# S5 layer's gated GEMM: last four tiles from plain fp32 to three fp32r products, two of their weight casts on GpSimd

## The chip, the cores and the metric

The kernel runs on one core of one Trainium2 chip. The metric is the device time of one execution in microseconds (us); smaller is better. A core has TensorE (matmuls, PE), VectorE (DVE), ScalarE (ACT), GpSimd (POOL) and SyncE (SP, which here issues most DMAs). Each engine takes its instructions in the order in which the program has them, and waits on semaphores for the others.

## The reference

Two layers on 256 tokens of width 2048: the first with differential attention, the second with an S5 state-space mixer, each followed by an MLP with squared relu. The change is in the S5 mixer's last step, the gated GEMM:

```
def s5_mixer(h, ..., d_skip, w_glu):
    ...                                   # complex diagonal scan over the sequence, giving y
    y = y + d_skip.astype(F32) * h.astype(F32)
    g = jax.nn.gelu(y).astype(h.dtype)
    val, gate = jnp.split(g @ w_glu, 2, axis=-1)
    return val * jax.nn.sigmoid(gate)
```

All is fp32. `g` is 256 x 2048 and `w_glu` 2048 x 4096.

## The kernel before

**Weights.** All weights come as one stream of chunks of 256 rows by 512 columns (512 KB, a tile `raw` of 128 x 2 x 512, five buffers). Elsewhere in the kernel a GEMM is made of fp32r products: `prep(i)` has ScalarE cast a chunk to fp32r (`wh`, L191), has VectorE subtract to get the remainder (`wl`, L113), and starts the next load with `load_next()`. `ktile` then makes three matmuls of each 128-row tile: high by high, high by low, low by high (L201 to L203). `wh` and `wl` have four buffers each.

**S5 stage.** `s5_phase` loops over 16 tiles of 128 channels. For tile j+1, `s5_e` makes matmuls on TensorE (L1040) and a chain of ten VectorE instructions, two of them scans (L1050), which gives the state `xp`. For tile j, `s5_y` makes the output matmuls on TensorE (L1073), then 16 gelu instructions on ScalarE (L1080), then the cast of `g` to fp32r into `blk.h` (L1084). Groups of `s5_y` are pairs of tiles but for the first two and the last two: (12,13), (14,), (15,). `s5_rest(j)` has VectorE subtract to get the low part `blk.l` of all groups up to j (in the trace a subtraction `x<-s2k,x` of L113); before the change it has lagged three tiles, and the last groups came after the last tile.

**The gated GEMM's first column block.** Inside this loop `glu_tile(j)` multiplies tile j of `g` with rows of `w_glu` for the first 512 columns of `val` (chunk `GLU0 + j//2*2`) and of `gate` (the chunk after it), for two halves of the tokens, into four PSUM accumulators. It takes `g` and `raw` as they are, in plain fp32 (L1106): four matmuls a tile, each of which the trace records as two. The order of work is written out by hand: tiles 0 to 12 are done inside the loop, three iterations behind (tile 12 in iteration 15), and 13, 14 and 15 after it. The other three column blocks follow as ordinary GEMMs of fp32r products, `gemm(glu_lhs)`, beginning with chunk GLU0+16. Between them `evict_val` copies the `val` accumulators (L1298) and `evict_gate` takes the sigmoid (L1305) and adds to the residual, which TensorE then transposes for the next MLP (L445).

Of the kernel before, what the change touches and what calls it, by code (L numbers as in the profile page):

```python
# [16 lines left out]
P = 128  # L17
# [5 lines left out]
KB = 4  # L23
# [14 lines left out]
NJ = 16  # L38
# [2 lines left out]
SLOTS_HOP = 3  # L41
WARM = (18, 4, 8)
LAG = 3


class Lhs:
# [11 lines left out]
def tile_trunk(  # L58
# [8 lines left out]
    act = nc.scalar  # L67
    pe = nc.tensor
    pool_e = nc.gpsimd
# [10 lines left out]
    def nm(s):  # L80
        uid[0] += 1
        return f"{s}_{uid[0]}"
# [15 lines left out]
    def bank():  # L98
        return ring("sd")

    def tmp(shape, tag, bufs=None, dt=F32):
        if bufs is None:
            return sb.tile(shape, dt, tag=tag, name=nm(tag))
        return sb.tile(shape, dt, tag=tag, name=nm(tag), bufs=bufs)
# [7 lines left out]
    def sub(o, a, b):  # L112
        v.tensor_tensor(out=o, in0=a, in1=b, op=ALU.subtract)  # L113

    def tsc(o, a, s1, op0, s2=None, op1=None):
        if op1 is None:
            v.tensor_scalar(out=o, in0=a, scalar1=s1, scalar2=None, op0=op0)
        else:
            v.tensor_scalar(out=o, in0=a, scalar1=s1, scalar2=s2, op0=op0, op1=op1)
# [11 lines left out]
    def pump():  # L131
        clock[0] += 1
        for g in list(side):
            if g[0] <= clock[0]:
                try:
                    d = next(g[1])
                    g[0] = clock[0] + (d if d else 1)
                except StopIteration:
                    side.remove(g)

    def until(cond):
        while not cond():
            assert side
            pump()


    stream = []
# [12 lines left out]
    raws, preps = {}, {}  # L160
    pos = [0]
    FINE = 2
    GLU0 = (12 + 4 + 32) * 8
    POOL = 6

    def load(i):
        if i >= len(stream) or i in raws:
            return
        r = wp.tile([P, WK, BW], F32, tag="raw", name=nm("raw"), bufs=RAW)
        if i < FINE:  # L170
            for k in range(WK):
                nc.sync.dma_start(r[:, k], stream[i][:, k])
        else:
            nc.sync.dma_start(r, stream[i])
        raws[i] = r

    def load_next():

        load(len(raws))

    def prep(i):
        if i >= len(stream) or i in preps or GLU0 <= i < GLU0 + 16:
            return
        r = raws[i]
        h = wp.tile([P, WK, BW], F32R, tag="wh", name=nm("wh"), bufs=LIVE)
        l = wp.tile([P, WK, BW], F32R, tag="wl", name=nm("wl"), bufs=LIVE)
        preps[i] = (h, l)
        step = 1 if i < FINE else WK
        for k in range(0, WK, step):
            sl = slice(k, k + step)  # L190
            act.copy(h[:, sl], r[:, sl])  # L191
            if FINE <= i < POOL:
                sub(l[:, 0], r[:, 0], h[:, 0].bitcast(F32))
                pool_e.tensor_tensor(out=l[:, 1], in0=r[:, 1], in1=h[:, 1].bitcast(F32), op=ALU.subtract)
            else:
                sub(l[:, sl], r[:, sl], h[:, sl].bitcast(F32))
        load_next()

    def ktile(accs, lhs, k, wh, wl, t, first, last):
        ts = slice(t * P, (t + 1) * P)  # L200
        pe.matmul(accs[t], lhs.h[:, k, ts], wh, start=first, stop=False)  # L201
        pe.matmul(accs[t], lhs.h[:, k, ts], wl, start=False, stop=False)  # L202
        pe.matmul(accs[t], lhs.l[:, k, ts], wh, start=False, stop=last)  # L203

    def ahead():
        for d in range(AHEAD + 1):
            prep(pos[0] + d)
# [16 lines left out]
    def new_accs():  # L224
        return [ring("acc") for _ in range(NT)]
# [94 lines left out]
    def keep_warm(n):  # L320

        if n == 0:
            return
        a = ring("acc")
        for _ in range(n):
            pe.matmul(a, x1[3].h[:, 0, 0:P], x1[3].h[:, 0:2], start=True, stop=True)
# [647 lines left out]
    glu_lhs = [Lhs() for _ in range(NB)]  # L974
    tab, U, X, G = {}, {}, {}, {}
    first_vals = []

    def s5_fetch(j):

        if j >= NJ or j in tab:  # L980
            return
        tag = "x" if j < 3 else "a"
        teo = lp.tile([P, 2, 2, Q, P], F32, tag=tag, name=nm("teo"))
        te, to = teo[:, 0], teo[:, 1]
        t2 = tmp([P, SCR - O_T], "t4", bufs=4)
        nc.sync.dma_start(te.rearrange("p i q c -> p (i q c)"), scr[j][:, O_E:O_O])
        nc.sync.dma_start(to.rearrange("p i q c -> p (i q c)"), scr[j][:, O_O:O_T])
        nc.sync.dma_start(t2, scr[j][:, O_T:])
        tab[j] = (te, to, t2[:, 0:Q * P].rearrange("p (q c) -> p q c", q=Q),
                  t2[:, Q * P:].rearrange("p (i q k) -> p i q k", i=2, q=Q))  # L990
# [11 lines left out]
    def s5_dk(j):  # L1002
        if j < NJ:
            act.copy(dks[j % 4][:, :, 1:], rr[:, j * Q:(j + 1) * Q, None].broadcast_to([P, Q, NCH - 1]))
# [22 lines left out]
    def s5_scale(j, factor):  # L1027
        u = U[j]
        uv = u.rearrange("p i q k -> p (i q) k")
        mult(uv, uv, factor[:, None, :].broadcast_to([P, 2 * Q, NCH]))  # L1030
        U[j], U[j + 1] = u[:, 0], u[:, 1]
# [59 lines left out]
    def s5_rest(j):  # L1091

        while rest and rest[0][0] <= j:
            _, blk, kk, n, g = rest.pop(0)
            sub(blk.l[:, kk:kk + n], g[:, 0:n], blk.h[:, kk:kk + n].bitcast(F32))
            blk.ready = kk + n == KB
# [2 lines left out]

    def glu_tile(j):  # L1100

        g = G.pop(j)
        c, kk = GLU0 + j // WK * 2, j % WK
        for i, accs in ((c, A["v"]), (c + 1, A["g"])):
            for t in range(NT):
                pe.matmul(accs[t], g[:, t * P:(t + 1) * P], raws[i][:, kk], start=j == 0, stop=j == NJ - 1)  # L1106
            if j == NJ - 1 and i == c:
                first_vals.extend(evict_val(accs))
            if kk == WK - 1:
                load_next()  # L1110
                pos[0] += 1

    def s5_phase(norm):
        until(lambda: norm.done)
        act.activation(warm_act, warm_act, AF.Gelu_apprx_tanh)
        keep_warm(WARM[0])
        sel = wp.tile([P, 2, NT, P], F32, tag="wl", name="sel", bufs=LIVE)
        ar, diag = sel[:, 0], sel[:, 1]
        for t in range(NT):
            tsc(ar[:, t], sela.rearrange("p s r -> p (s r)"), norm.rstd[:, t:t + 1], ALU.mult)  # L1120
            act.activation(diag[:, t], ident, AF.Copy, scale=norm.rstd[:, t:t + 1])
        prs = bank()[:, 0:NCH]
        for t in range(NT):
            pe.matmul(prs, ar[:, t], selb[:, t], start=(t == 0), stop=(t == NT - 1))
        keep_warm(WARM[1])
        s5_scale(0, prs)
        s5_scale(2, prs)
        s5_e(0)
        for j in (4, 6):
            for _ in s5_u(j, diag, "acc"):  # L1130
                pass
        groups = [(0,), (1,), (2, 3), (4, 5), (6, 7), (8, 9), (10, 11), (12, 13), (14,), (15,)]
        ys = {}
        for grp in groups:
            gen = s5_y(grp)
            for j in grp:
                ys[j] = (gen, j == grp[-1])
        glu = 0
        for j in range(NJ):
            if j + 1 < NJ:  # L1140
                s5_e(j + 1)
            s5_rest(j - 3)
            if j < 2:
                keep_warm(WARM[2])
            if j in (2, 3) or j >= 2 + LAG:
                if glu == 0:
                    A["v"], A["g"] = new_accs(), new_accs()
                glu_tile(glu)
                glu += 1
            gen, end = ys[j]  # L1150
            next(gen)
            s5_dk(j + 4)
            if end:
                for _ in gen:
                    pass
            if j in (2, 4, 6, 8):
                for _ in s5_u(j + 6, diag):
                    pass
            s5_fetch(j + 4)
            pump()  # L1160
        while glu < NJ:
            prep(GLU0 + 16 + glu - NJ + LAG)
            glu_tile(glu)
            glu += 1
        s5_rest(NJ)


    x0 = [Lhs() for _ in range(NB)]
# [1 line left out]
    for b in range(NB):  # L1170
        spawn(xT_block(x0[b], b, 0, norm0, wait=10), 3 * b)
    pump()
    prep(0)
    until(lambda: x0[0].ready)

# [118 lines left out]
    def evict_val(accs):  # L1294
        vs = []
        for t in range(NT):
            n = tmp([P, BW], "vsb", bufs=4)
            act.copy(n, accs[t])  # L1298
            vs.append(n)
        return vs  # L1300
# [75 lines left out]
```

## Time and profile before

| | us |
|---|---|
| median of 3 runs | 2105.34 (2104.72 to 2105.79) |
| the profiled execution | 2103.02 |
| its span, first to last instruction | 2101.2 |
| PE busy (share of the span) | 2076.6 (99%) |
| DVE busy | 1372.2 (65%) |
| ACT busy | 1059.8 (50%) |
| POOL busy | 123.1 (6%) |

Shares of busy time are means over the whole program. What the change is worth is read in the S5 stage, about 1130 to 1250 us, from what each engine waits for there.

### The profile page before, as it was taken

How to read it: one execution, taken by the hardware profiler on the slowest of the kernel's cores; microseconds unless marked ns; L12 is line 12 of the kernel's file. 1: busy time of each engine (PE TensorE's matmuls, PEld its weight loads, DVE VectorE, ACT ScalarE, POOL GpSimd, SP SyncE). 2: the span in 40 equal slices, each digit the busy share in tenths (PEclk: the TensorE clock that was granted, in tenths of full speed). 3: DMA queues.
4: the chain of work that ended last, by engine and by line, in shares of the span. 5: the costliest groups of instructions: out<-in, count | busy, mean ns of one | idle time of the engine just before them, and what ended most of it. 6: DMA issues, size and time to landing. Idle time of an engine off the chain costs nothing.

```text
span 2101.2 us, 31797 instructions
## 1 busy us (share of the span) xinstructions
PE 2076.6 (99%) x12126; PEld 1763.2 (84%) x12126; DVE 1372.2 (65%) x2310; ACT 1059.8 (50%) x1634; POOL 123.1 (6%) x210
## 2 busy tenths in 40 slices
PE   8999999999999999999999999999999999999998
PEld 8899998888888888888887658888888888888886
DVE  5775656688678767767866865565546645645655
ACT  6445545555445544454565874444434434434443
POOL 2000200021020002100110000000000000000000
PEclk9999999999999999999999999999999999999999
DMA  7467765687776777677677855566565556555653
GB/s 249 157 194 237 251 179 178 215 234 266 237 244 224 280 236 224 229 269 233 215 268 296 288 204 190 191 202 197 191 194 189 189 191 191 182 200 180 201 191 130
DMA packets 230813, 452.57 MB, mean 215 GB/s; under 512 B 20818, under 2 KB 29348, under 8 KB 230660
## 3 DMA queue, kind: packets, MB, share of 16 engines
q1 hardware_dynamic: 218400, 416.34, 59.7%
q0 software_dynamic: 11440, 32.86, 4.8%
q8 instruction: 95, 1.56, 0.3%
q10 hardware_dynamic: 820, 1.34, 0.2%
q14 instruction: 58, 0.48, 0.1%
HBM read 420.85 MB, written 41.68 MB: 220 GB/s over the span
## 4 chain that ended last, share of the span: by engine, by line
PE 94%; DVE 2%; DMA 2%; ACT 1%; issue 0%; SPq 0%; ACTq 0%
PE acc L265 21%; PE acc L201 16%; PE acc L203 16%; PE acc L202 16%; PE acc L269 11%; PE acc L248 3%; PE acc L250 3%; PE acc L249 3%; PE acc L1106 2%; PE y L1073 1%; DVE wl L113 1%; ACT s2k L1080 1%; PE sd L1040 1%; DMA raw<-in_mlp_w_dram 1%; PE sd L445 0%
## 5 line engine op out<-in xcount | busy, mean ns | idle before, releaser
L113 DVE TENSOR_TENSOR wl<-raw,wh 128x1024 fp32r<-128x1024 f32 (+1 forms) x690 | 833.2, 1217 | 580.2 <-ACT wh L191 575.6
L191 ACT CAST wh<-raw 128x1024 fp32r<-128x1024 f32 (+1 forms) x690 | 713.4, 1047 | 639.4 <-PE acc L203 351.3
L201 PE MATMUL acc<-wh,x 128*128 128x512 f32 x832 | 326.8, 393 | 0.0
L203 PE MATMUL acc<-wh,x 128*128 128x512 f32 x832 | 324.0, 389 | 0.0
L202 PE MATMUL acc<-wl,x 128*128 128x512 f32 x832 | 323.9, 389 | 0.0
L265 PE MATMUL acc<-x,wh 128*128 128x512 f32 x1024 | 273.9, 394 | 2.3 <-DVE s2k L110 2.3
L265 PE MATMUL acc<-a,wh 128*128 128x512 f32 x1024 | 272.8, 393 | 0.0
L201 PE MATMUL acc<-wh,a 128*128 128x512 f32 x640 | 251.4, 393 | 0.0
L203 PE MATMUL acc<-wh,a 128*128 128x512 f32 x640 | 249.3, 389 | 0.0
L202 PE MATMUL acc<-wl,a 128*128 128x512 f32 x640 | 249.2, 389 | 0.0
L265 PEld LDWEIGHTS acc<-x,wh 128*128 128x128 f32 x1024 | 177.2, 189 | 28.5 <-DVE s2k L110 2.7
L265 PEld LDWEIGHTS acc<-a,wh 128*128 128x128 f32 x1024 | 177.3, 189 | 25.3 <-ACT s2k L1305 0.4
L203 PEld LDWEIGHTS acc<-wh,x 128*128 128x128 f32 x832 | 156.1, 188 | 32.7
L202 PEld LDWEIGHTS acc<-wl,x 128*128 128x128 f32 x832 | 156.2, 188 | 32.2 <-issue 0.2
L201 PEld LDWEIGHTS acc<-wh,x 128*128 128x128 f32 x832 | 156.2, 188 | 32.0 <-ACT vsb L1298 0.2
L269 PEld LDWEIGHTS acc<-a,wl 128*128 128x128 f32 x1024 | 152.8, 190 | 18.7
L269 PEld LDWEIGHTS acc<-x,wl 128*128 128x128 f32 x1024 | 152.4, 190 | 18.8
L269 PE MATMUL acc<-x,wl 128*128 128x256 f32 x1024 | 158.0, 282 | 0.0
L269 PE MATMUL acc<-a,wl 128*128 128x256 f32 x1024 | 157.5, 281 | 0.0
L248 PE MATMUL acc<-x,wh 128*128 128x256 f32 x512 | 148.4, 290 | 1.2 <-ACT wh L191 1.2
L250 PE MATMUL acc<-x,wl 128*128 128x256 f32 x512 | 145.5, 284 | 0.0
L249 PE MATMUL acc<-x,wh 128*128 128x256 f32 x512 | 145.4, 284 | 0.0
(242 smaller groups left out, 2107.9 us busy)
## 6 DMA issues: line engine op xcount, KB each, us to landing
raw<-in_mlp_w_dram SPq DMA_DIRECT2D x512, 512.0 KB
raw<-in_a_w_in_dram SPq DMA_DIRECT2D x94, 512.0 KB
raw<-in_b_w_glu_dram SPq DMA_DIRECT2D x64, 512.0 KB
raw<-in_a_w_out_dram SPq DMA_DIRECT2D x32, 512.0 KB
scr<-t POOLq DMA_DIRECT2D x32, 512.0 KB, 5.7
teo<-scr SPq DMA_DIRECT2D x32, 512.0 KB
t<-scr SPq DMA_DIRECT2D x16, 512.0 KB
pwr<-pwn SPq DMA_DIRECT2D x16, 256.0 KB
```

Of the source, the lines that this page charges most:

```text
L113: v.tensor_tensor(out=o, in0=a, in1=b, op=ALU.subtract)
L191: act.copy(h[:, sl], r[:, sl])
L201: pe.matmul(accs[t], lhs.h[:, k, ts], wh, start=first, stop=False)
L202: pe.matmul(accs[t], lhs.h[:, k, ts], wl, start=False, stop=False)
L203: pe.matmul(accs[t], lhs.l[:, k, ts], wh, start=False, stop=last)
L248: pe.matmul(o, wh[:, kk, cs], lhs.h[:, k], start=f and c % 2 == 0, stop=False)
L249: pe.matmul(o, wh[:, kk, cs], lhs.l[:, k], start=False, stop=False)
L250: pe.matmul(o, wl[:, kk, cs], lhs.h[:, k], start=False, stop=e and c % 2 == 1)
L265: pe.matmul(a[c], wh, lhs.hl[:, k].rearrange("p i s -> p (i s)"), start=first, stop=False)
L269: pe.matmul(a[c][:, S:], wl, lhs.h[:, k], start=False, stop=last)
L1040: pe.matmul(pe_[h, i, q], te[:, i, q, h], u[:, q], start=True, stop=True)
L1106: pe.matmul(accs[t], g[:, t * P:(t + 1) * P], raws[i][:, kk], start=j == 0, stop=j == NJ - 1)
```

## The change

Tiles 12 to 15 of the first column block are done as fp32r products (48 matmuls by `ktile` in place of 16 plain ones). For that, chunks GLU0+12 to GLU0+15 go through `prep`: 12 and 13 at the end of iteration 13, 14 and 15 at the end of iteration 15, the casts of the latter two on GpSimd. `s5_rest` runs one tile less late in the last iteration, and ahead of each tile after the loop. The `prep` of chunks 16 to 18 moves from ahead of tiles 13 to 15 to behind them. The next load is now started by `prep` for the four chunks, not by the tile.

```diff
@@ prep
-        if i >= len(stream) or i in preps or GLU0 <= i < GLU0 + 16:
+        if i >= len(stream) or i in preps or GLU0 <= i < GLU0 + WHOLE:
...
-            act.copy(h[:, sl], r[:, sl])
+            if GLU0 + 14 <= i < GLU0 + 16:
+                pool_e.tensor_copy(h[:, sl], r[:, sl])
+            else:
+                act.copy(h[:, sl], r[:, sl])
@@ glu_tile
-        g = G.pop(j)
+        g, blk = G.pop(j), glu_lhs[j // KB]
...
-                pe.matmul(accs[t], g[:, t * P:(t + 1) * P], raws[i][:, kk], start=j == 0, stop=j == NJ - 1)
+                if i in preps:
+                    wh, wl = preps[i]
+                    ktile(accs, blk, j % KB, wh[:, kk], wl[:, kk], t, j == 0, j == NJ - 1)
+                else:
+                    pe.matmul(accs[t], g[:, t * P:(t + 1) * P], raws[i][:, kk], start=j == 0, stop=j == NJ - 1)
...
-                load_next()
+                if i in preps:
+                    del preps[i]
+                else:
+                    load_next()
@@ s5_phase, loop over j
-            s5_rest(j - 3)
+            s5_rest(j - 3 if j < NJ - 1 else j - 2)
...
             s5_fetch(j + 4)
+            if j == 13:
+                for i in (12, 13):
+                    prep(GLU0 + i)
+            if j == NJ - 1:
+                for i in (14, 15):
+                    prep(GLU0 + i)
             pump()
         while glu < NJ:
+            s5_rest(glu)
+            glu_tile(glu)
             prep(GLU0 + 16 + glu - NJ + LAG)
-            glu_tile(glu)
             glu += 1
-        s5_rest(NJ)
```

`WHOLE` is 12. In the changed file the lines of these functions stand 4 to 18 lower.

First place: VectorE, behind the state chain of tile 14 (whose last instruction writes `bc_11353`). The rows before are the chain of tile 15, which ends with the two writes of `bc_11357`, then the low part of `g` for tiles (10,11), then the remainders of chunks 16 and 17.

```order
L110 TENSOR_TENSOR bc_11353<-s2k_12906,s2k_12907 128x4x63
L107 TENSOR_TENSOR c_2268_12976<-sd_12959,t_2251_12812 128x512 x2
L110 TENSOR_TENSOR c_2268_12976<-c_2268_12976 128x256
L113 TENSOR_TENSOR c_2268_12976<-c_2268_12976 128x256
L1050 SCALAR_TENSOR_TENSOR s2k_12981<-s1k_11356,c_2268_12976 128x256 x2
L107 TENSOR_TENSOR s2k_12984<-s2k_12981,t_2251_12812 128x8x63
L107 TENSOR_TENSOR s2k_12985<-s2k_12981,t_2251_12812 128x8x63
L113 TENSOR_TENSOR bc_11357<-s2k_12984,s2k_12985 128x4x63
L110 TENSOR_TENSOR bc_11357<-s2k_12984,s2k_12985 128x4x63
L113 TENSOR_TENSOR x_12655<-s2k_12793,x_12655 128x2x256
L113 TENSOR_TENSOR wl_13090<-raw_12997,wh_13089 128x1024
L113 TENSOR_TENSOR wl_13104<-raw_13093,wh_13103 128x1024
```

Of the change, the same place: the remainders of chunks 12 and 13 (`wl_12960`, `wl_12966`) stand ahead of the chain of tile 15, which is otherwise the same.

```order
L111 TENSOR_TENSOR bc_11353<-s2k_12906,s2k_12907 128x4x63
L114 TENSOR_TENSOR wl_12960<-raw_12700,wh_12959 128x1024
L114 TENSOR_TENSOR wl_12966<-raw_12850,wh_12965 128x1024
L108 TENSOR_TENSOR c_2274_12988<-sd_12971,t_2251_12812 128x512 x2
L111 TENSOR_TENSOR c_2274_12988<-c_2274_12988 128x256
L114 TENSOR_TENSOR c_2274_12988<-c_2274_12988 128x256
L1054 SCALAR_TENSOR_TENSOR s2k_12993<-s1k_11356,c_2274_12988 128x256 x2
L108 TENSOR_TENSOR s2k_12996<-s2k_12993,t_2251_12812 128x8x63
L108 TENSOR_TENSOR s2k_12997<-s2k_12993,t_2251_12812 128x8x63
L114 TENSOR_TENSOR bc_11357<-s2k_12996,s2k_12997 128x4x63
L111 TENSOR_TENSOR bc_11357<-s2k_12996,s2k_12997 128x4x63
```

Second place: VectorE right behind that chain, of the change. `x_12655` is the low part for tiles (10,11); `x_12957` are those of (12,13), of 14 and of 15; the `wl` rows are the remainders of chunks 14, 15, 16, 17 and 18 in turn. Before, the three rows of `x_12957` stood behind the remainder of chunk 18.

```order
L114 TENSOR_TENSOR x_12655<-s2k_12793,x_12655 128x2x256
L114 TENSOR_TENSOR x_12957<-s2k_12940,x_12957 128x2x256
L114 TENSOR_TENSOR wl_13111<-raw_12854,wh_13110 128x1024
L114 TENSOR_TENSOR wl_13117<-raw_12963,wh_13116 128x1024
L114 TENSOR_TENSOR wl_13135<-raw_12969,wh_13134 128x1024
L114 TENSOR_TENSOR x_12957<-s2k_13036,x_12957 128x256
L114 TENSOR_TENSOR wl_13154<-raw_13005,wh_13153 128x1024
L114 TENSOR_TENSOR x_12957<-s2k_13092,x_12957 128x256
L114 TENSOR_TENSOR wl_13177<-raw_13009,wh_13176 128x1024
```

The low part for tile 14 now has the remainder of chunk 16 ahead of it, and that for tile 15 the remainder of chunk 17.

Third place: ScalarE, of the change, from the gelu of pair (12,13) on. The first two `L195` rows are the casts of chunks 12 and 13, which were not there before; the others are chunks 16, 17 and 18.

```order
L1084 ACTIVATE s2k_12940<-y_12856 32x128 x16
L1088 CAST x_12957<-s2k_12940 128x2x256
L195 CAST wh_12959<-raw_12700 128x1024
L195 CAST wh_12965<-raw_12850 128x1024
L1084 ACTIVATE s2k_13036<-y_13011 32x64 x16
L1088 CAST x_12957<-s2k_13036 128x256
L1084 ACTIVATE s2k_13092<-y_13067 32x64 x16
L1088 CAST x_12957<-s2k_13092 128x256
L195 CAST wh_13134<-raw_12969 128x1024
L195 CAST wh_13153<-raw_13005 128x1024
L1316 COPY vsb_13166<-acc_11991 128x512
L1316 COPY vsb_13168<-acc_11992 128x512
```

Behind these come the cast of chunk 18 and then the table load for the sigmoid; before, all three casts stood ahead of the two copies.

## Rows read from the trace of the kernel before

**Rows 1.** The page's chain that ended last: share of the span by engine.

```profile
PE 94%; DVE 2%; DMA 2%; ACT 1%; issue 0%; SPq 0%; ACTq 0%
```

**Rows 2.** Waits of PE, whole span: waited for, us in total, times, longest.

```profile
PE acc L1106 <- ACT s2k L1080: 4.5, 3, 2.2
```

**Rows 3.** Timeline of PE, 1195 to 1270 us: start, duration, what, idle before.

```profile
1224.66 0.34 PE L1073 MATMUL y<-vsb,t 128*64 128x64 f32 x4
...
1232.93 3.70 PE L1106 MATMUL acc<-raw,s2k 128*128 128x512 f32 x8 [0.54 <-ACT s2k L1080]
...
1238.11 10.57 PE L1106 MATMUL acc<-raw,s2k 128*128 128x512 f32 x24
...
1248.75 0.39 PE L202 MATMUL acc<-wl,x 128*128 128x512 f32 x1
...
1253.28 0.55 PE L445 MATMUL sd<-ident,xres 128*128 128x128 f32 x3 [1.00 <-DVE xres L110]
...
1262.34 0.39 PE L201 MATMUL acc<-wh,x 128*128 128x512 f32 x1
...
1269.82 0.39 PE L201 MATMUL acc<-wh,x 128*128 128x512 f32 x1
```

**Rows 4.** Timeline of ACT, 1214 to 1262 us.

```profile
1226.33 6.55 ACT L1080 ACTIVATE s2k<-y 32x128 f32<-32x128 f32 x16 [4.99 <-PE y L1073]
1232.91 0.62 ACT L1084 CAST x<-s2k 128x512 fp32r<-128x512 f32 x1
...
1238.60 4.59 ACT L1080 ACTIVATE s2k<-y 32x64 f32<-32x64 f32 x16
...
1243.53 1.99 ACT L191 CAST wh<-raw 128x1024 fp32r<-128x1024 f32 x2
...
1249.85 1.09 ACT L1305 ACTIVATE s2k<-acc 128x512 f32<-128x512 f32 x2
```

**Rows 5.** Timeline of DVE, 1214 to 1262 us.

```profile
1215.04 1.29 DVE L107 TENSOR_TENSOR c<-sd,t 128x512 f32<-128x512 f32 x2 [0.75 <-PE sd L1040]
...
1220.32 0.68 DVE L113 TENSOR_TENSOR x<-s2k,x 128x512 fp32r<-128x512 f32 x1
...
1227.26 1.29 DVE L107 TENSOR_TENSOR c<-sd,t 128x512 f32<-128x512 f32 x2 [0.75 <-PE sd L1040]
...
1232.75 0.69 DVE L113 TENSOR_TENSOR x<-s2k,x 128x512 fp32r<-128x512 f32 x1
1244.60 2.36 DVE L113 TENSOR_TENSOR wl<-raw,wh 128x1024 fp32r<-128x1024 f32 x2 [11.16 <-ACT wh L191]
...
1248.62 1.36 DVE L113 TENSOR_TENSOR x<-s2k,x 128x512 fp32r<-128x512 f32 x3
```

**Rows 6.** Groups of POOL by line: busy us, mean ns, idle before.

```profile
L194 POOL TENSOR_TENSOR wl<-raw,wh 128x512 fp32r<-128x512 f32 x4 | 7.1, 1781 | 15.2 <-ACT wh L191 15.2
...
L1332 POOL TENSOR_TENSOR xres<-xres,vsb 128x512 f32<-128x512 f32 x2 | 2.5, 1268 | 992.7 <-ACT junk L421 992.7
```

**Rows 7.** Windows of 1 us: engines' busy us, PEclk, DMA share, GB/s.

```profile
1230.00:1231.00 1.00, 1.00 (x8) 0.24 (x9) 0.97 (x3) 0.98 (x3) 0.00 (x0) 1.00 0.77 246
...
1234.00:1235.00 1.00, 1.00 (x4) 0.47 (x3) 0.00 (x0) 0.95 (x5) 0.00 (x0) 1.00 0.28 96
```

**Rows 8.** Timeline of PE, 0 to 32 us, and 1134 to 1160 us.

```profile
7.65 0.58 PE L248 MATMUL acc<-x,wh 128*128 128x256 f32 x1 [1.25 <-ACT wh L191]
...
10.04 0.41 PE L248 MATMUL acc<-x,wh 128*128 128x256 f32 x1
10.25 0.41 PE L249 MATMUL acc<-x,wh 128*128 128x256 f32 x1
...
11.88 0.28 PE L250 MATMUL acc<-x,wl 128*128 128x256 f32 x1
12.00 0.28 PE L248 MATMUL acc<-x,wh 128*128 128x256 f32 x1
...
1150.18 3.70 PE L1106 MATMUL acc<-raw,s2k 128*128 128x512 f32 x8 [1.81 <-ACT s2k L1080]
```

More of the change, by code (lines that the diff above doesn't have):

```diff
@@ L43 @@
 LAG = 3
+WHOLE = 12
 class Lhs:
```

## The prediction

> **What bounds the kernel now.** I read the chain that ended last first: 94% of it is TensorE [rows 1]. So the kernel is a stream of matmuls, and only two things can move it: how long TensorE computes, and how long it waits. The list of its waits comes next. In the S5 stage before the change it waits for little: 4.5 us in all for gelu results, the longest 2.2 us [rows 2]. Then I read the timelines of TensorE, ScalarE and VectorE from 1214 to 1262 us, where the changed tiles lie. I count tiles from 0 to 15. In the loop over j, tile 12 runs in iteration 15, and tiles 13, 14 and 15 follow the loop. The reader is to see three things. TensorE starts tile 12 at 1232.93, after 0.54 us of waiting, and tiles 13 to 15 at 1238.11 without a wait. The next block's second product starts at 1248.75 [rows 3]. ScalarE is full from 1226.33 on: the gelu of pair (12,13) takes 6.55 us, then its cast, the gelus of 14 and of 15, and at 1243.53 the first weight cast [rows 4]. VectorE runs the state chain of tile 15 from 1227.26, so that it is over soon after 1232.75, and then has nothing until 1244.60 (11.16 us idle) [rows 5].
>
> **What TensorE saves.** A plain fp32 tile takes four matmuls of 512 columns, each recorded as two. Tiles 13 to 15 end, for the product that follows, at 1248.75 − 0.23 = 1248.52: (1248.52 − 1238.11)/3 = 3.47 us each [rows 3]. Tile 12 took about the 3.63 us that its 3.70 us row leaves as pitch. In three parts a tile is 12 fp32r matmuls. Their pitch is (1269.82 − 1262.34)/33 = 0.2267 us, from the first and last of 34 products in a row [rows 3], so 2.72 us. Four tiles: 14.04 − 10.88 = 3.2 us less computing. That is the whole gain on offer, 0.15% of the time; a measurement of this kernel can tell about 0.2% (4.2 us) from no change.
>
> **What the change adds in front of tile 12.** Work for chunks 12 and 13 is written at the end of iteration 13, behind the gelu of (12,13). Both engines take their work in order. So:
>
> 1. ScalarE casts 12 and 13 after the pair's own cast, which starts at 1232.91 and takes 0.62: from 1233.53 on [rows 4]. Two casts take 1.99 us, and VectorE's first subtraction starts 1.07 us after the first cast does (1243.53 to 1244.60) [rows 4, 5]. So the subtraction of chunk 12 starts at 1234.61, however early its weights landed.
> 2. On VectorE both subtractions stand ahead of the state chain of tile 15. The two take 2.36 us, with 0.05 of overlap into the next, 2.3 us [rows 5]. The chain therefore starts at about 1236.9 instead of 1227.26; behind the waiting subtraction its ten instructions stand still for nearly ten microseconds.
> 3. The chain takes 5.28 us up to the subtraction behind it (1215.04 to 1220.32, the same chain of an earlier tile) [rows 5]: 1242.2. Next are the low parts of g for tiles (10,11) and then, moved up one iteration, for (12,13): 128x512 each, 1.36 us for the two by the three of 1248.62, where one is 128x512 and two are half that [rows 5]. They end at 1243.5, call it 1243.6 with the hand-over.
> 4. Tile 12 needs that low part in its third matmul. TensorE can do the first two at 1234.6 and 1235.8, and then stands until 1243.6. Before, tile 12 had begun at 1232.93.
>
> **From there to tile 15.** Ten matmuls remain in tile 12: 2.27 us, to 1245.9. The output matmuls of tile 15 come behind them on TensorE. The gelu starts 1.67 us after such a group (1224.66 to 1226.33) [rows 3, 4], so at 1247.55. From its start to the next weight cast on ScalarE is 4.93 us (1238.60 to 1243.53) [rows 4]: chunk 16 is cast at 1252.5. Here the second wait lies. On VectorE the subtraction of chunk 16 now stands ahead of the low part of g for tile 14, because that chunk is prepared right after tile 13. It starts at 1253.55 and takes 1.15 us, the low part (half of 0.69) about 0.4 us: 1255.15. TensorE is through the outputs by the time that the gelu starts, finishes tile 13 at 1247.5 + 2.72 = 1250.2, does two matmuls of tile 14, and waits some 4.5 us. Tile 15's own low part, behind chunk 17's subtraction, is there by 1256.7 and its third matmul only comes at 1257.9, so it waits no more. From tile 14's third matmul to the next block's second product are 23 pitches, 5.2 us: 1260.36 against 1248.75, **11.6 us later**, gain of the faster tiles included.
>
> **Smaller terms.** The cast of chunk 18 now stands between the copies of the first accumulators and the sigmoid's table load. Before, the sigmoid ran at 1249.85, 1.33 us after tile 15's end [rows 4]. Now: copies end 0.3 us before the end of tile 15, cast 1.05, table load 1.28, so the sigmoid starts 2.0 us after. TensorE waits on that path already (1.00 us at its second transpose [rows 3]), so the 0.7 us count in full. The loads of chunks 15 and 16 leave as before, when tile 11 gives their buffers free. Those of 17 to 20 wait on subtractions instead of tiles; 17 and 18 leave earlier than before (1236 against about 1241). No byte is added and no DMA wait is on the path, so I cost this at nothing; if weights were late again, the cover would be the subtractions that are queued anyway.
>
> **GpSimd's casts.** No row shows a GpSimd cast. The nearest are its 128x512 subtraction, 1.78 us, and a 128x512 product, 1.27 us [rows 6]; for 128x1024 between nothing and 3.56 us. Chunk 15 comes with 16 in the traffic that begins by 1230 and is over before 1235 [rows 7]. The cast is then done by 1238.6 at the latest, and VectorE wants it at 1243.6: hidden. What it may do to VectorE is another matter. GpSimd's subtractions, which the code issues in one breath with a VectorE subtraction of the same size, take 0.51 us longer than its products at the end of the program [rows 6]. The Trainium skill (SBUF — State Buffer, Who interferes with whom) says that a VectorE instruction with two SBUF inputs and a GpSimd instruction that reads SBUF exclude each other, the later one waiting. The 0.51 us agree. By that rule a long cast of chunk 15 would hold the subtraction of chunk 12, which is on the path. I take 0, since chunk 15 is the first of the two loads and VectorE has nothing to do just then, and keep 3.6 us as the upper end. Chunk 14's cast comes beside the chain of tile 14, whose result TensorE wants only about 4 us after the chain's end.
>
> **TensorE's clock after a stand of 7.8 us.** The nearest answer in the middle of the program: after 1.81 us of waiting a tile runs its 3.70 us as ever [rows 8], so nothing. The other end is the start of the program: the 256-column products stand 0.21 us apart at 10.04 and 0.12 apart at 11.88 [rows 8], which are the levels 1.2 and 2.4 GHz. The slow stretch begins with the first product at 7.65 and ends between 10.25 and 11.88 [rows 8]; taken to 11.4, it is 3.7 us of work in which half is lost, 1.9 us. The long stand, with two single matmuls in it, is nearer to the start than to 1.8 us: I take 1.9. The second, 4.5 us, is nearer to 1.8: I take 0 and keep 1.9. The Trainium skill (TensorE: Matmul & The Clock Gate, Why this matters for your kernels) warns against idle gaps between bursts of matmuls, since the clock falls to half. By that rule both stands would cost; no row before shows it in the middle of the program.
>
> **Sum.** 11.6 + 0.7 + 1.9 = 14.2 us. The profiled execution took 2103.02 us (span 2101.2); it would be 2117.2. It is 2.3 us below the median of the runs, 2105.34, and I put the difference on the median: **2119.5 us**, 0.67% slower.
>
> **Rivals.**
> - *Clock never falls:* 12.3 us, 2117.6. For it: no wait in the S5 stage has shown a fall. Chance 0.22.
> - *Clock falls at both stands:* 16.1 us, 2121.4. For it: both are longer than any wait that a row shows at full pace. Chance 0.22. The rule of the Trainium skill on the clock, named above, would give this case.
> - *GpSimd's cast holds VectorE* for its upper end on the path: 14.2 + 3.6 = 17.8 us, 2123.1. Against it: VectorE idles when the chunk lands. Chance 0.06. The rule of the Trainium skill on the shared port, named above, is this case.
> - *No second wait:* if the low part of tile 14 came before chunk 16's subtraction, only the gelu of tile 15 would be late. Its cast ends at 1252.6, its low part at 1253.0, eleven pitches later the next block's second product: 1255.5, so 6.7 + 0.7 + 1.9 = 9.3 us, 2114.6. Against it stands the order on VectorE. Chance 0.04.
> - *Not slower:* the split of chunks 12 and 13 keeps nothing waiting, and 3.2 − 0.7 = 2.5 us are gained: 2102.8. It is decided by ScalarE: its casts would have to be over when the chain of tile 14 leaves VectorE, near 1226.6, about 9 us before they can be. Every microsecond that the two casts come earlier gives one back. Nothing in the profile speaks for it but VectorE's 11.16 us of idleness, which lies too late. Chance 0.04.
>
> **How the numbers follow.** One fall of the clock keeps 0.42 and gives the predicted time. The range 2114.5 to 2123.5 holds every case but the last, with room for a microsecond of spread and for a slow stretch that is longer than at the start. Not slower is 0.04 by the last rival, mostly within 0.2%, since 2.5 us are below it; I leave 0.02 for a gain I don't see.
>
> **What would show it.** In the changed profile: a wait of TensorE at its third fp32r matmul of tile 12 of about 8 us, ended by VectorE; VectorE's subtraction at 1234.6 with an idle stretch of some 8 us before it and the chain of tile 15 behind it; a second wait of 4 to 5 us in tile 14; pitches near 0.45 us behind the first stand if the clock fell; no such pitches behind the second. Wrong would be the prediction if VectorE began that chain near 1227, or if weight casts came before the gelu of (12,13).

## The result and the profile after

| | before | changed |
|---|---|---|
| median, us (4 runs each) | 2105.57 (2104.72 to 2106.74) | 2121.55 (2120.68 to 2122.01) |
| ratio to before | | 1.007, 95% interval 1.0058 to 1.0083 |
| profiled execution, us (span) | 2103.02 (2101.2) | 2121.49 (2119.7) |
| granted TensorE clock, mean | 0.998 | 0.995 |

The changed kernel is slower by 16.0 us between the medians, or 0.8%; by the ratio's interval it is 0.6 to 0.8%. The forecast was 14.2 us. In the changed file all lines named here stand one or more lower, so L113 is L114, L203 is L207 and so on.

TensorE's waits from 1200 to 1275 us in the changed kernel: who waited, for whom, us in total, times, longest.

```profile
PE acc L207 <- DVE x L114: 11.3, 2, 7.1
PE acc L205 <- ACT wh L195: 2.1, 1, 2.1
PE sd L449 <- DVE xres L111: 1.9, 2, 1.0
PE acc L206 <- DVE wl L114: 0.8, 1, 0.8
```

Its timeline on TensorE in the same place. The first row is the state matmuls of tile 15, which stood at 1226.11 before: the trace is 3.09 us late already when it comes here. That difference arose where the two programs still do the same: 1.63 us of it were there at tile 0 (1151.81 against 1150.18 [rows 8]), and the other 1.46 come at tile 2, shown below.

```profile
1229.20 1.10 PE L1044 MATMUL sd<-vsb,teo 128*64 128x64 f32 x32
...
1237.56 0.49 PE L205 MATMUL acc<-wh,x 128*128 128x512 f32 x1 [2.07 <-ACT wh L195]
1238.82 0.49 PE L206 MATMUL acc<-wl,x 128*128 128x512 f32 x1 [0.77 <-DVE wl L114]
1246.43 0.79 PE L207 MATMUL acc<-wh,x 128*128 128x512 f32 x1 [7.12 <-DVE x L114]
1247.02 0.63 PE L205 MATMUL acc<-wh,x 128*128 128x512 f32 x1
1247.44 0.63 PE L206 MATMUL acc<-wl,x 128*128 128x512 f32 x1
...
1250.66 0.34 PE L1077 MATMUL y<-vsb,t 128*64 128x64 f32 x4
...
1255.31 0.39 PE L206 MATMUL acc<-wl,x 128*128 128x512 f32 x1
1259.93 0.50 PE L207 MATMUL acc<-wh,x 128*128 128x512 f32 x1 [4.23 <-DVE x L114]
...
1266.86 0.39 PE L206 MATMUL acc<-wl,x 128*128 128x512 f32 x1
...
1271.75 0.55 PE L449 MATMUL sd<-ident,xres 128*128 128x128 f32 x3 [1.00 <-DVE xres L111]
```

The reader sees both stands (a stand is a longer wait of TensorE): 7.12 us at the third product of tile 12 and 4.23 us at the third product of tile 14, each ended by a low part of g from VectorE. Behind the first the products stand 0.43 us apart instead of 0.23. From the state matmuls to 1266.86, the next block's second product, are 37.66 us; before it was 22.64 (1226.11 to 1248.75 [rows 3]). To the second transpose it is 42.55 against 27.17 us: 15.4 us of the 16.0 are here. The spans of the two profiled executions differ by 18.5 us; the 3.09 and these 15.38 make 18.47 of it, so next to nothing is lost behind.

VectorE in the same stretch:

```profile
1227.54 1.93 DVE L108 TENSOR_TENSOR s2k<-s2k,t 128x504 f32<-128x504 f32 x2
...
1229.84 0.41 DVE L111 TENSOR_TENSOR bc<-s2k,s2k 128x252 f32<-128x252 f32 x1
1237.54 2.36 DVE L114 TENSOR_TENSOR wl<-raw,wh 128x1024 fp32r<-128x1024 f32 x2 [7.28 <-ACT wh L195]
1239.81 1.28 DVE L108 TENSOR_TENSOR c<-sd,t 128x512 f32<-128x512 f32 x2
...
1245.09 1.29 DVE L114 TENSOR_TENSOR x<-s2k,x 128x512 fp32r<-128x512 f32 x2
...
1258.31 1.23 DVE L114 TENSOR_TENSOR wl<-raw,wh 128x1024 fp32r<-128x1024 f32 x1 [9.67 <-ACT wh L195]
1259.45 0.42 DVE L114 TENSOR_TENSOR x<-s2k,x 128x256 fp32r<-128x256 f32 x1
```

It is idle for 7.28 us with the state chain of tile 15 queued behind a subtraction that waits for ScalarE, and for 9.67 us with the low part of tile 14 queued behind chunk 16. Before, that chain began right behind its matmuls [rows 5]. What it waits for is on ScalarE:

```profile
1229.42 6.49 ACT L1084 ACTIVATE s2k<-y 32x128 f32<-32x128 f32 x16 [4.97 <-PE y L1077]
1235.94 0.62 ACT L1088 CAST x<-s2k 128x512 fp32r<-128x512 f32 x1
1236.46 1.99 ACT L195 CAST wh<-raw 128x1024 fp32r<-128x1024 f32 x2
...
1252.32 4.57 ACT L1084 ACTIVATE s2k<-y 32x64 f32<-32x64 f32 x16 [8.84 <-PE y L1077]
1256.93 0.40 ACT L1088 CAST x<-s2k 128x256 fp32r<-128x256 f32 x1
1257.24 1.99 ACT L195 CAST wh<-raw 128x1024 fp32r<-128x1024 f32 x2
```

The casts of 12 and 13 come behind the gelu of their pair, as ordered, and chunk 16's behind the gelu of 15, which itself waited for tile 12. Windows of the changed kernel: engines' busy us with counts, then the granted clock (PEclk), DMA share, GB/s.

```profile
1244.00:1248.00 4.00, 1.57 (x4) 1.28 (x5) 3.97 (x7) 0.00 (x0) 0.00 (x0) 0.50 0.02 4
...
1252.00:1257.00 5.00, 3.69 (x24) 2.68 (x20) 0.00 (x0) 4.47 (x17) 0.00 (x0) 1.00 0.10 39
...
1260.00:1263.00 3.00, 3.00 (x8) 2.41 (x9) 1.34 (x2) 0.00 (x0) 0.00 (x0) 0.57 0.69 201
```

The clock is at half its level behind each stand, and back in between.

In the S5 stage it had fallen once before, outside the changed part. Tile 2 of the gated GEMM is plain fp32 in both programs. Before the change, and in the changed kernel:

```profile
1169.43 3.70 PE L1106 MATMUL acc<-raw,s2k 128*128 128x512 f32 x8 [2.15 <-ACT s2k L1080]
```

```profile
1171.05 5.40 PE L1115 MATMUL acc<-raw,s2k 128*128 128x512 f32 x8 [1.78 <-ACT s2k L1084]
```

The second trace waited less, and yet the tile took 1.70 us longer, at a granted clock of 0.50 from 1172 to 1175; in the first the clock stayed at 1.00. In the eleven traces of this case the same tile waits 1.78 to 2.18 us. It takes 3.70 us in two of them (before and e2) and 5.32 to 5.40 us in the other nine.

GpSimd's two casts:

```profile
1226.91 1.43 POOL L193 CAST wh<-raw 128x1024 fp32r<-128x1024 f32 x1 [126.41 <-DMA raw<-in_b_w_glu_dram]
1235.83 1.04 POOL L193 CAST wh<-raw 128x1024 fp32r<-128x1024 f32 x1 [7.49 <-DMA raw<-in_b_w_glu_dram]
```

They take 1.43 and 1.04 us and are done long before they are wanted.

### The profile page after: what moved, and what is told of

Same layout as the page of the kernel before. It is cut to its first block, busy times and chain, and to the rows that moved or that the text cites. A ratio compares the mean times of both kernels' runs of the same rounds, so it can differ in the third digit from the quotient of the medians.

```text
span 2119.7 us, 31841 instructions
## 1 busy us (share of the span) xinstructions
PE 2079.6 (98%) x12142; PEld 1769.5 (83%) x12142; DVE 1377.5 (65%) x2314; ACT 1060.9 (50%) x1636; POOL 125.4 (6%) x212
## 5 line engine op out<-in xcount | busy, mean ns | idle before, releaser
L114 DVE TENSOR_TENSOR wl<-raw,wh 128x1024 fp32r<-128x1024 f32 (+1 forms) x694 | 838.3, 1217 | 592.1 <-ACT wh L195 589.6
L195 ACT CAST wh<-raw 128x1024 fp32r<-128x1024 f32 (+1 forms) x692 | 715.2, 1047 | 639.1 <-PE acc L207 344.7
L207 PE MATMUL acc<-wh,x 128*128 128x512 f32 x848 | 331.9, 391 | 11.3 <-DVE x L114 11.3
L205 PE MATMUL acc<-wh,x 128*128 128x512 f32 x848 | 334.2, 394 | 2.1 <-ACT wh L195 2.1
L206 PE MATMUL acc<-wl,x 128*128 128x512 f32 x848 | 331.6, 391 | 0.8 <-DVE wl L114 0.8
L207 PE MATMUL acc<-wh,a 128*128 128x512 f32 x640 | 249.3, 390 | 0.0
L207 PEld LDWEIGHTS acc<-wh,x 128*128 128x128 f32 x848 | 160.1, 189 | 45.9 <-DVE x L114 12.1
L205 PEld LDWEIGHTS acc<-wh,x 128*128 128x128 f32 x848 | 160.1, 189 | 34.8 <-ACT wh L195 2.2
```

## The experiments

My theory: two instructions that wait in VectorE's queue hold work that TensorE needs, first the subtraction of chunk 12 ahead of the state chain, then that of chunk 16 ahead of a low part; the clock's fall behind each stand is added. Rivals: ScalarE's added casts, GpSimd's casts, the moved preparation of chunks 16 to 18, or the fp32r form of the products.

The experiments ran on three chips, on which the kernel before spreads from 2103.0 to 2112.4 us. So ratios to it on the same chip are given with their intervals, and beside them the stretch in the trace from the state matmuls of tile 15 to the next block's second transpose (27.17 us before, 42.55 changed; 27.19 in e6, whose work there is that of the kernel before).

| kernel | ratio to before, 95% interval | stretch, us |
|---|---|---|
| changed | 1.0070 (1.0058 to 1.0083) | 42.55 |
| e6, moves only | 0.9996 (0.9988 to 1.0004) | 27.19 |
| e2, low parts first | 1.0050 (1.0037 to 1.0063) | 36.39 |
| e1, subtractions behind the chain | 1.0031 (1.0019 to 1.0043) | 35.39 |
| e3, both orders | 1.0011 (1.0001 to 1.0021) | 29.62 |
| e4, TensorE kept at work | 1.0058 (1.0046 to 1.0071) | 39.27 |
| e5, four casts on GpSimd | 1.0041 (1.0028 to 1.0055) | 38.55 |
| e8, e3 with TensorE kept at work | 1.0006 (0.9997 to 1.0015) | 28.13 |
| e9, e3 with chunk 18 later | 1.0005 (0.9996 to 1.0014) | 28.71 |
| e7, work spread | 0.9988 (0.9979 to 0.9998) | 26.00 |

**e6, only the moves.** The last four tiles stay plain; nothing is split.

```diff
-WHOLE = 12
+WHOLE = 16
```

> Only the moves of the change: the last four tiles stay plain fp32 and nothing of chunks 12 to 15 is split or cast; the low parts of g come earlier and chunks 16 to 18 are prepared behind the tiles. Theory (the waits come from the new casts and subtractions on ScalarE and VectorE): plain tiles need no low part, so no stand; only the sigmoid starts up to 0.7 us later and the rest is the kernel before, 2105.6 to 2106.5. Rival (the moved preparation of chunks 16 to 18 makes the next block late): 5 us or more over before, with waits in the next block's first products.

The same as before (27.19 against 27.17 us), and TensorE's waits are those of before, 0.6 and 1.5 us. The moved `prep` calls and low parts cost nothing by themselves. The 0.7 us forecast on the sigmoid's path don't show here: the plain second half of tile 15 leaves ScalarE time for the cast of chunk 18 between the copies, over at 1251.85, and the table load at 1252.81. e9 comes back to it.

**e2, low parts of tiles 14 and 15 ahead of the remainders of 16 and 17.**

```diff
+        s5_rest(NJ)
         while glu < NJ:
-            s5_rest(glu)
             glu_tile(glu)
```

> The changed kernel with the low parts of tiles 14 and 15 ahead of the remainders of chunks 16 and 17 on VectorE. Theory: the second stand (4.2 us) and the second slow stretch (1.7 us) go, the first stand of 7.1 us stays; about 6.3 us less than the changed kernel, near 2115.2. Rival (tile 14 waits for ScalarE's gelu or for chunk 14's cast, not for its place behind chunk 16): no change, 2121.5.

The stretch falls by 6.16 us; 6.3 was expected. The second stand is gone and the first stays:

```profile
PE acc L207 <- DVE x L114: 7.0, 1, 7.0
PE sd L449 <- DVE xres L111: 2.3, 2, 1.3
```

So tile 14 waited for its place in VectorE's queue, not for gelu or weights. By the ratio it is some 4 us. Behind the transposes, which wait 2.3 us here, the clock fell (0.52 from 1264.7 to 1267.9), and those products lie outside the stretch.

**e1, the subtractions of 12 and 13 behind the state chain of tile 15.** The casts stay.

```diff
             if j == 13:
                 for i in (12, 13):
-                    prep(GLU0 + i)
+                    half_cast(GLU0 + i, act)      # the cast of prep
...
             s5_rest(j - 3 if j < NJ - 1 else j - 2)
+            if j == NJ - 1:
+                for i in (12, 13):
+                    half_sub(GLU0 + i)            # the subtraction and the next load
```

> The changed kernel with the subtractions of chunks 12 and 13 behind the state chain of tile 15 instead of ahead of it; the casts stay where they are. Theory: the first stand of 7.1 us shrinks to under 2 us in total and its slow stretch goes; the gelu of 15 then starts right behind that of 14, so tile 14's third product comes 8.9 us earlier: near 2112.6, with the second stand and its slow stretch still there. Rival (ScalarE's casts ahead of the gelu of 14 are what delays everything): under 3 us less, 2118.5 or more.

The stand of 7.12 us is gone; what is left ahead of tile 12 is 2.2 and 1.0 us. The stretch falls by 7.16 instead of 8.9 us, because the products of tile 12 are slow all the same (0.43 us apart). ScalarE's casts ahead of the gelu of 14, the rival, are still there and would have kept nearly all of the loss.

**e3, both orders.**

> Both of the two orders above. Theory: no stand over 3 us, the clock stays up, the next block's second product comes 15.4 us earlier than in the changed kernel: near 2106.1, the same as before within 0.2%. Rival (something else in the change costs, such as GpSimd's casts or the fp32r products themselves): 2110 or more.

The stretch is 29.62 us, 12.9 less than in the changed kernel but 2.45 more than before, where I expected no loss. No stand is over 2.2 us, and yet the clock did not stay up. Timeline of e3 on TensorE and its windows:

```profile
1239.75 0.50 PE L217 MATMUL acc<-wh,x 128*128 128x512 f32 x1 [2.14 <-ACT wh L208]
1241.29 0.50 PE L218 MATMUL acc<-wl,x 128*128 128x512 f32 x1 [1.03 <-DVE wl L114]
1241.62 0.53 PE L219 MATMUL acc<-wh,x 128*128 128x512 f32 x1
1241.95 0.63 PE L217 MATMUL acc<-wh,x 128*128 128x512 f32 x1
1242.38 0.63 PE L218 MATMUL acc<-wl,x 128*128 128x512 f32 x1
```

```profile
1241.60:1245.30 3.70, 3.70 (x11) 2.82 (x9) 3.04 (x3) 3.56 (x13) 0.00 (x0) 0.54 0.75 239
1245.30:1258.20 12.90, 12.90 (x98) 10.41 (x96) 4.49 (x6) 11.11 (x27) 0.00 (x0) 1.00 0.47 151
...
1262.30:1265.30 3.00, 3.00 (x11) 2.41 (x10) 2.01 (x4) 1.88 (x3) 0.00 (x0) 0.50 0.62 175
```

It fell behind two waits of 2.14 and 1.03 us with one product between them, and again behind the transposes, which wait 1.30 and 1.00 us here. That part of my theory had the wrong size: I had taken waits of some 2 us as free.

**e4, the changed kernel with TensorE kept at work in both stands.** The added products go into a PSUM bank that nobody reads.

```diff
+    def fill(n):
+        a, b = bank(), glu_lhs[0]
+        for _ in range(n):
+            pe.matmul(a, b.h[:, 0, 0:P], b.h[:, 0:2], start=True, stop=True)
...
+                if j == NJ - 1:
+                    fill(46)
                 glu_tile(glu)
...
             s5_rest(glu)
+            if glu == NJ - 2:
+                fill(19)
             glu_tile(glu)
```

> The changed kernel with 46 products of 512 columns that nobody reads ahead of tile 12 and 19 ahead of tile 14, so that TensorE works through both stands. Theory (the clock falls because TensorE stands): the products behind the stands keep 0.227 us apart, 1.96 and 1.72 us are saved: near 2117.9, granted clock near 0.998. Rival (the slow products come from late operands or from the fp32r form): no change, 2121.5, or slower if the added products push tile 12.

The stretch falls by 3.28 us; 3.68 is what the slow products of the changed kernel had cost. The granted clock is 1.00 behind both stands:

```profile
1249.50:1256.80 7.30, 7.30 (x73) 5.81 (x72) 2.65 (x3) 2.62 (x10) 0.00 (x0) 1.00 0.47 144
...
1261.10:1270.00 8.90, 8.63 (x37) 6.49 (x35) 4.03 (x7) 4.87 (x7) 0.00 (x0) 1.00 0.43 126
```

So the slow products are the clock's, and neither late operands nor the fp32r form.

**e5, the casts of 12 and 13 on GpSimd too, in the same place.**

```diff
-            if GLU0 + 14 <= i < GLU0 + 16:
+            if GLU0 + 12 <= i < GLU0 + 16:
```

> The changed kernel with the casts of chunks 12 and 13 on GpSimd too, at the same place of the program. Theory: VectorE's subtractions no longer wait for ScalarE's gelu of (12,13) and its casts; they start right behind the chain of tile 14, the first stand shrinks to 3 to 4 us, the gelu of 15 follows that of 14, and the second stand stays: near 2112.6. Rival (GpSimd's casts take the port from VectorE so that its chains get longer by what the casts take): 2115 or more.

Only 4.0 us less than the changed kernel; 8.9 was expected. The subtraction no longer waits for ScalarE, but VectorE's chains are longer. e5 on GpSimd and VectorE:

```profile
1228.73 1.04 POOL L193 CAST wh<-raw 128x1024 fp32r<-128x1024 f32 x1 [8.83 <-DMA raw<-in_b_w_glu_dram]
1230.01 1.13 POOL L193 CAST wh<-raw 128x1024 fp32r<-128x1024 f32 x1 [0.24 <-DMA raw<-in_b_w_glu_dram]
1238.08 1.27 POOL L193 CAST wh<-raw 128x1024 fp32r<-128x1024 f32 x1 [6.94 <-DVE s2k L1054]
```

```profile
1228.19 2.11 DVE L1054 TENSOR_TENSOR_SCAN s2k<-s1k,c 128x256 f32<-128x256 f32 x2
1230.34 1.93 DVE L108 TENSOR_TENSOR s2k<-s2k,t 128x504 f32<-128x504 f32 x2
...
1238.55 1.93 DVE L108 TENSOR_TENSOR s2k<-s2k,t 128x504 f32<-128x504 f32 x2
```

The two scans take 1.27 us elsewhere in the same trace and the two products 1.28: each GpSimd cast that falls beside them adds 0.65 to 0.84 us. Two of them put off the subtractions, and the third, of chunk 15, lies in the state chain of tile 15. TensorE still stood 1.31 us ahead of tile 12, 3.06 us in it and 4.23 us in tile 14, and the clock fell behind the last two. The theory's mechanism held, the rival's too, and both were needed for the size.

**e8, e3 with 14 idle products ahead of tile 12** (`fill(14)` as in e4).

> Both orders of the experiment before, and 14 products that nobody reads ahead of tile 12. Theory (waits of 2.1 and 1.0 us with one product between them already bring TensorE's clock down): the slow products of tile 12 go, 1.7 us are saved, the stretch from the state matmuls of tile 15 to the next block's second transpose falls from 29.62 to about 27.9 us; the slow products behind the transposes stay. Rival (those products were slow because VectorE's subtractions came in piecemeal): 29.6 us again.

28.13 us, 1.49 less than e3, with no wait ahead of tile 12's products and no slow ones there. The slow products behind the transposes stay.

**e9, e3 with the cast of chunk 18 left to the next block.**

```diff
-            prep(GLU0 + 16 + glu - NJ + LAG)
+            if glu < NJ - 1:
+                prep(GLU0 + 16 + glu - NJ + LAG)
```

> Both orders, and the cast of chunk 18 behind the sigmoid instead of ahead of its table load. Theory: the transposes wait 0.7 to 1.3 us less, so the clock does not fall behind them; the same stretch falls by 0.7 to 1.3 us to about 28.5, and about 1.3 us more are saved behind it; the total is that of the kernel before within 0.1%. Rival (the sigmoid is late because of the accumulators' copies): no change in the waits.

28.71 us, 0.91 less. The transposes wait 1.4 us in all instead of 2.3, and the products behind them are fast again. So that cast was the cost on the sigmoid's path. The 1.49 us of e8 and these 0.91 make 2.40 of the 2.45 us that e3 had over the kernel before; no run has both.

**e7, the split tiles with their work spread.** Against the changed kernel: four casts on GpSimd; chunk 12 prepared in iteration 12; the subtraction of 13 behind the state chain of tile 15; low parts of 14 and 15 first; chunk 18 as in e9; and on TensorE the outputs of tile 15 ahead of tile 12:

```diff
             if j in (2, 3) or j >= 2 + LAG:
+                if j == NJ - 1:
+                    next(ys[j][0])
                 glu_tile(glu)
```

> Split tiles with the work spread: four casts on GpSimd, chunk 12 prepared one iteration earlier, the subtraction of 13 behind the chain of tile 15, the outputs of tile 15 ahead of tile 12 on TensorE, low parts of 14 and 15 ahead of chunks 16 and 17, chunk 18 behind the sigmoid. Theory: no stand over 2.5 us, tile 15 waits only for its gelu: 1 to 3 us less than the kernel before, 2103 to 2105. Rival (the gelu of 15, not TensorE, bounds this stretch, so fp32r brings nothing): the same as before, 2105.5.

26.00 us, 1.17 less than before; the ratio is 0.9988 (0.9979 to 0.9998), some 2.5 us. It beats the changed kernel clearly, and the kernel before by less than the 0.2% that one comparison can usually tell. TensorE's waits in e7:

```profile
PE y L1089 <- DVE bc L114: 1.4, 1, 1.4
PE sd L461 <- DVE xres L111: 1.0, 1, 1.0
PE y L1089 <- ACT s2k L1096: 0.6, 1, 0.6
PE acc L219 <- DVE x L114: 0.3, 1, 0.3
```

The clock stays at 1.00 here. Of the 3.2 us that the products can save, waits of 2.0 us on the way to the outputs of tile 15 are still given back. Three of GpSimd's casts lie in the state chain of tile 14, whose scans and products take 2.28 us longer than elsewhere in the trace:

```profile
1226.15 2.06 DVE L1066 TENSOR_TENSOR_SCAN s2k<-s1k,c 128x256 f32<-128x256 f32 x2
1228.25 2.77 DVE L108 TENSOR_TENSOR s2k<-s2k,t 128x504 f32<-128x504 f32 x2
```

The chain of tile 15, for which TensorE waits 1.4 us, follows right behind. Without these casts there that wait should go; no run shows it.

## Why the prediction was right, and where a size was off

Times of the changed kernel less the 3.09 us by which it was late on arrival:

| step | forecast | measured |
|---|---|---|
| subtraction of chunk 12 starts | 1234.61 | 1234.45 |
| state chain of tile 15 starts | 1236.9 | 1236.72 |
| third product of tile 12 | 1243.6 | 1243.34 |
| outputs of tile 15, with 1.9 for the clock | 1247.8 | 1247.57 |
| third product of tile 14, with the same | 1257.05 | 1256.84 |
| next block's second product, with the same | 1262.26 | 1263.77 |

- **The two queues.** The casts behind the gelu, the chain behind the subtraction, the low part of 14 behind chunk 16: each stood where the forecast had it, within 0.3 us. e1 and e2 take them away one at a time, and e6 shows that the rest of the change is free. Without the clock the stretch to the next block's second product is longer by 15.02 − 1.96 − 1.72 = 11.34 us, for which the forecast had 11.6: right by its mechanism.
- **The clock at the first stand.** Ten products took 1250.66 − 1246.43 = 4.23 us instead of 2.27: 1.96 us, forecast 1.9. e4 shows that it is the clock.
- **The clock at the second stand** is the term that was mis-sized: 0 was taken, because 4.5 us seemed nearer to the 1.81 us wait of [rows 8] than to the start of the program. From 1259.93 to 1266.86 are 6.93 us for 23 products, 5.21 at full pace: 1.72 us. That is the rival in which the clock falls twice, 2121.4 us forecast. e3 shows how the choice failed: waits of 2.14 and 1.03 us are enough. And the one row of a wait at full pace said less than it seemed to: at tile 2 the clock fell behind 1.78 us of waiting in the changed kernel, and in nine of eleven traces. The profile before, with its 2.2 us of [rows 2] at full pace, is one of the other two. The rule on gaps from the Trainium skill (TensorE: Matmul & The Clock Gate, Why this matters for your kernels), weighed in the forecast, agrees with both stands of the changed kernel, 7.12 and 4.23 us. The gaps that it names are longer than the 1.78 us that were enough at tile 2; there the measurement decides.
- **The sigmoid's path** cost 0.36 us more, for 0.7. The mechanism is shown by e9, which puts the cast of chunk 18 behind the sigmoid and gets 0.91 us back.
- **GpSimd's casts** cost nothing on the path here: 1.43 us beside the chain of tile 14, which had room, and 1.04 us while VectorE was idle. The hold that the forecast kept as a rival is real: in the changed kernel the pair of products of L108 at 1227.54 took 1.93 us instead of 1.28, and in e5 it came onto the path. The Trainium skill (SBUF — State Buffer, Who interferes with whom) has the two engines exclude each other for instructions of this kind; the longer rows of e5 agree (2.11 and 1.93 us instead of 1.27 and 1.28).
- **What the products saved** was not measured by itself. In e3 tiles 13 to 15 run without a wait from 1247.14 to 1255.43, 8.29 us, against 10.41 before [rows 3]: 2.1 us less, where the forecast's rates give 2.25 for these three. There the waits and the slow products of tile 12 take it back; e7 keeps part of it.

The sum came out 1.8 us short of the medians' 16.0. The second fall, 1.72 us, was left out; the other three terms measured 11.34, 1.96 and 0.36 us, 0.5 less than forecast; and 0.6 us of the 16.0 lie outside the stretch, within the spread of the medians. So that the median meets the 2121.4 us of the rival within 0.2 us is in part luck: that rival's sum is 16.1 us, where the stretch shows 15.4. The range of 9 us was wide enough for nearly every case, so the total alone doesn't tell them apart; the rows do.

## What to carry to other kernels

Before you add work to an engine off the critical path, look at what stands behind it in that engine's queue: an instruction that waits holds everything after it, and here 2.3 us of subtractions, waiting for their casts, put off a 5.3 us chain by nearly ten. Place new work behind what the bound engine wants next, not where its own inputs are named. And price a stand of TensorE as the wait and the slow products behind it, even for a wait of about 2 us; that one trace shows none of them slow is no proof.

## What the runs showed of the hardware that was not expected

- TensorE's granted clock fell to half behind short waits: 2.14 and 1.03 us with a single product between them (e3: 0.54 from 1241.6 to 1245.3), 1.30 and 1.00 us at the transposes (e3: 0.50 from 1262.3 to 1265.3), and a single wait of 1.78 us at tile 2 (changed kernel: 0.50 from 1172 to 1175). It did not fall behind 0.91 and 1.00 us at the transposes of the changed kernel, nor behind 1.4 us in two waits there in e9, nor behind 2.15 us at tile 2 before. At tile 0 a wait of 1.8 us brought it down in none of the eleven traces. So the length of the wait alone does not decide it. Most falls cost 1.5 to 2 us; those of e5 cost 2.3 and 2.6.
- A GpSimd cast of 128x1024 from fp32 to fp32r took 1.04 us with VectorE idle, 1.43 beside it in the changed kernel, where the forecast, from two-input instructions [rows 6], had allowed up to 3.56. It adds 0.65 to 0.84 us to a pair of VectorE scans or products of two SBUF inputs beside it (e5).
